# Queries and keys of an attention layer transposed on VectorE, ahead of time, instead of on TensorE when they are used

## The chip, the cores and the metric

The kernel runs on one core of a Trainium2 chip. The metric is the device time of one execution in microseconds; the time of a kernel is the median of its runs. Five engines work side by side, each through its own instructions in order: TensorE (PE in the profile, PEld its weight loads), VectorE (DVE), ScalarE (ACT), GpSimd (POOL) and SyncE (SP), which here issues nearly all DMA transfers. Semaphores make an engine wait for another or for a transfer.

## The reference

One layer of a hybrid model, 16 meta tokens ahead of 1024 tokens of width 1024. One input projection feeds three mixers: a short convolution, a latent attention with 8 heads (MLA), and a retention with 4 heads. An output projection and a residual end the layer. Only the attention's queries and keys are touched by the change:

```python
def mla_mixer(c_q, c_kv, k_rope, z, q_a_norm, w_uq, kv_a_norm, w_ukv, q_norm, k_norm, cos, sin):
    q = (rms_norm(c_q, q_a_norm) @ w_uq).reshape(B, L, MLA_HEADS, QK_HEAD)          # QK_HEAD = 96
    ...
    k = jnp.concatenate([k_nope, k_r], axis=-1)
    q = rms_norm(q, q_norm)
    k = rms_norm(k, k_norm)
    q = jnp.concatenate([q[..., :QK_NOPE], apply_rope(q[..., QK_NOPE:], cos, sin)], axis=-1)
    k = jnp.concatenate([k[..., :QK_NOPE], apply_rope(k[..., QK_NOPE:], cos, sin)], axis=-1)
    ...
        s = jnp.einsum('bqhd,bkhd->bhqk', qb, k).astype(jnp.float32) * scale
        mask = cid[None, :] <= qc[:, None]
        s = jnp.where(mask[None, None], s, neg)
        p = jax.nn.softmax(s, axis=-1).astype(v.dtype)
        return jnp.einsum('bhqk,bkhd->bqhd', p, v)
    ...
    return o * jax.nn.silu(z)

u = rms_norm(h, ln_w[l])
(cx, cb, cc, cz, cq, ckv, krope, mz, rq, rk, rv, rz) = jnp.split(u @ w_in[l], IN_OFFSETS, axis=-1)
y = jnp.concatenate([y_conv, y_mla, y_ret], axis=-1)
h = h + y @ w_out[l]
```

## The kernel before, in words

Precision: every large product is made of three fp32r matmuls (`mm3`, L112) of high and low halves. `split` (L103 to L107) makes the halves: ScalarE writes the high one, VectorE (for some weights GpSimd) the low one by subtraction.

The program goes through units, each a block of columns of the input projection with eight weight chunks (`load_w`, L118: a DMA of 256 KB into one of three staging buffers, then a split):
- `mz`, the gate of the attention, in the opening (0 to 55 us), while the input arrives in pieces (`xs`) and is split. The row norms of the tokens come from ScalarE's sums of squares; `rps` (L243) spreads them over the partitions by a matmul with `dg`, once for each half of the tokens. The gated blocks `mzz` are stored to `mz_s` (L260).
- `A`, the latents of the attention (58 to 123 us): for each of nine tiles of tokens it makes q, k (`kqo`) and v, norms and rotates them, and stores them to HBM, token by token, in `q_s`, `k_s` (L388, L368) and `v_s`.
- `r0` and `r1`, the retention (120 to 246 us): nine tiles of tokens each. `r_proj` makes the projection, `r_rope` rotates on VectorE (`qk`), `r_score` makes the scores `rsp` on TensorE, which VectorE decays into `qs` (L478), and updates the running `state`; `r_out` (L494) multiplies `qs` on TensorE into `rop`. `later` and `step` put each part one tile behind the one before it, so that tile t's projection stands between the parts of tiles t-1, t-2 and t-3.
- `c0` and `c1`, the convolution (246 to 343 us).
- the attention (from 325 us, mixed with the end of c1): 8 heads of 8 query tiles. `score` makes S and its row maxima, `p_t` transposes the probabilities, `attend` multiplies them by v; `partial` does the first quarter of the output projection between them.
- the output projection's end (531 us on).

Queries and keys return in pairs of heads: `load_pair` (L546, L547) gathers 768 KB each of q and k, still one token to a partition. S needs them with the 96 features of a head on the partitions, so `qk_t` transposes them on TensorE, four transposes of 128 tokens (L668) into a PSUM tile, and splits that tile into `qT` or `kT`; the scale `wqk` (the product of the two norms' weights) is applied to q there. `qk_t` is called two heads ahead, four times a head: two halves of the tokens, q and k.

A scheduler sets the order of each engine's instructions from the order of the code and its own estimates of time; once built the order is fixed. Buffers come from pools: the pool of q, k and `kqo` tiles has two buffers for each tag, and a tile waits until the one two before it under its tag has been used.

## Time and profile before

| | us |
|---|---|
| median of 3 runs | 580.92 |
| lowest and highest | 580.18, 584.61 |
| profiled execution, its own time | 581.55 |
| its span | 579.8 |
| TensorE busy | 569.8 (98%) |
| VectorE busy | 330.9 (57%) |
| ScalarE busy | 255.0 (44%) |
| GpSimd busy | 224.1 (39%) |

The profile is of one execution; its span leaves out what lies before the first and behind the last instruction. The granted TensorE clock is at full speed in all 40 slices of the page. A row of the timeline gives start, length, engine, line, operation, the tile written and the tiles read, how many instructions were joined in the row, and in brackets how long the engine had been idle before and what ended that.

### The profile page before, as it was taken

What the parts mean: (1) busy time and instruction counts of PE and PEld (TensorE: products, weight loads), DVE (VectorE), ACT (ScalarE), POOL (GpSimd) and SP (SyncE); (2) the same over time, 40 slices, a digit from 0 to 9 for tenths busy, and PEclk for the clock granted to TensorE, in tenths of its full rate; (3) what the DMA queues carried; (4) which work ended last, traced back from release to release, by engine and by line L of the source; (5) the groups of instructions that cost most, each with busy time, mean ns of one, the idle gap of its engine ahead of it and who ended that gap; (6) DMA issues with size and microseconds to landing.
All of it is one profiled execution on the core that took longest, in us unless ns stands there. A gap on an engine that the chain in (4) does not pass through costs nothing.

```text
span 579.8 us, 9595 instructions
## 1 busy us (share of the span) xinstructions
PE 569.8 (98%) x3401; PEld 481.7 (83%) x3401; DVE 330.9 (57%) x761; ACT 255.0 (44%) x616; POOL 224.1 (39%) x330
## 2 busy tenths in 40 slices
PE   8999999999999999999999999999999999999997
PEld 5877899988888888898898888898888888876886
DVE  5547768888536432553332667675757857664132
ACT  6765535665234332532010438475655646543000
POOL 2023258677103220151242968443524334624000
PEclk9999999999999999999999999999999999999999
DMA  8887513274703200130030648235112223113096
GB/s 326 289 265 241 182 67 120 108 224 158 234 1 92 74 0 19 54 110 18 20 97 1 199 145 273 73 103 171 56 38 73 77 71 128 37 68 116 1 301 224
DMA packets 46657, 70.39 MB, mean 121 GB/s; under 512 B 3792, under 2 KB 21840, under 8 KB 46480
## 3 DMA queue, kind: packets, MB, share of 16 engines
q1 hardware_dynamic: 43008, 63.47, 33.8%
q10 hardware_dynamic: 3600, 6.29, 2.9%
q8 instruction: 27, 0.44, 0.3%
q14 instruction: 22, 0.18, 0.1%
HBM read 48.75 MB, written 21.00 MB: 120 GB/s over the span
## 4 chain that ended last, share of the span: by engine, by line
PE 83%; DMA 9%; DVE 3%; ACT 2%; issue 2%; POOL 0%; SPq 0%; DVEq 0%; ACTq 0%; POOLq 0%
PE r L112 16%; PE S L112 9%; PE cv L112 8%; PE part L112 7%; PE A L112 6%; PE o L765 6%; PE pTp L724 5%; PE cz L112 4%; PE cb L112 4%; DMA out<-ot 4%; PE out L112 3%; PE qps L112 3%; DMA xs<-in_xT 2%; DMA xt<-in_x 2%; PE rsp L477 1%
## 5 line engine op out<-in xcount | busy, mean ns | idle before, releaser
L702 ACT ACTIVATE pr<-S,smx 128x144 f32<-128x144 f32 (+8 forms) x72 | 50.4, 701 | 27.3 <-DVE smx L693 13.4
L693 DVE TENSOR_REDUCE smx<-S 128x1 f32<-128x144 f32 (+8 forms) x72 | 49.8, 701 | 15.7 <-PE S L112 6.3
L710 POOL TENSOR_SCALAR pm<-pr,smx 128x16 f32<-128x16 f32 x64 | 18.4, 288 | 85.2 <-DVE smx L708 61.3
L711 POOL TENSOR_SCALAR pr<-pr,smx 128x128 f32<-128x128 f32 (+3 forms) x64 | 48.1, 752 | 0.6 <-DVE smx L708 0.6
L724 PE MATMUL pTp<-ident,pr 128*128 128x128 f32 x288 | 45.4, 274 | 1.5 <-ACT pt L730 1.4
L730 ACT COPY pt<-pTp 128x512 f32<-128x512 f32 (+2 forms) x64 | 31.8, 505 | 26.3 <-PE pTp L724 24.9
L451 POOL TENSOR_SCALAR kw<-qk,con 128x64 f32<-128x64 f32 (+1 forms) x36 | 13.8, 397 | 71.7 <-DVE qk L447 58.4
L724 PEld LDWEIGHTS pTp<-ident,pr 128*128 128x128 f32 x288 | 35.0, 140 | 7.0 <-POOL wol L104 1.8
L765 PEld LDWEIGHTS o<-pt,v 128*64 128x64 f32 x448 | 26.5, 137 | 12.1 <-issue 4.7
L765 PE MATMUL o<-pt,v 128*64 128x256 f32 (+2 forms) x448 | 36.2, 309 | 0.0
L112 PE MATMUL r<-wh_r,xal 128*128 128x512 f32 (+1 forms) x80 | 30.5, 381 | 0.0
L112 PE MATMUL r<-wh_r,xah 128*128 128x512 f32 (+1 forms) x80 | 30.4, 380 | 0.0
L112 PE MATMUL part<-woh,yh 128*128 128x512 f32 x64 | 30.1, 470 | 0.0
L112 PE MATMUL r<-wl_r,xah 128*128 128x512 f32 (+1 forms) x80 | 30.0, 375 | 0.0
L882 DVE SCALAR_TENSOR_TENSOR ot<-out,xr 128x512 f32<-128x512 f32 (+1 forms) x17 | 11.2, 660 | 31.1 <-DMA out<-ot 16.8
L112 PE MATMUL r<-wl_r,xbh 128*128 128x512 f32 x64 | 26.1, 409 | 0.0
L112 PE MATMUL r<-wh_r,xbh 128*128 128x512 f32 x64 | 25.7, 401 | 0.0
L112 PE MATMUL part<-wol,yh 128*128 128x512 f32 x64 | 25.5, 399 | 0.0
L112 PE MATMUL r<-wh_r,xbl 128*128 128x512 f32 x64 | 25.5, 398 | 0.0
L112 PE MATMUL part<-woh,yl 128*128 128x512 f32 x64 | 25.2, 394 | 0.0
L773 DVE TENSOR_TENSOR ym<-o,ym 64x256 f32<-64x256 f32 x32 | 13.5, 421 | 16.7 <-PE o L767 16.2
L104 POOL TENSOR_TENSOR wol<-wos,woh 128x512 fp32r<-128x512 f32 x16 | 20.4, 1291 | 2.6 <-ACT woh L103 2.6
(295 smaller groups left out, 1716.1 us busy)
## 6 DMA issues: line engine op xcount, KB each, us to landing
xt<-in_x SPq DMA_DIRECT2D x16, 256.0 KB, 4.5
ws_r<-in_win SPq DMA_DIRECT2D x16, 256.0 KB, 3.3
ws_c<-in_win SPq DMA_DIRECT2D x16, 256.0 KB, 2.9
wos<-in_wout SPq DMA_DIRECT2D x16, 256.0 KB, 3.8
xp<-in_x SPq DMA_DIRECT2D x16, 256.0 KB, 2.7
p_s<-xp SPq DMA_DIRECT2D x16, 256.0 KB, 2.0
xr<-p_s SPq DMA_DIRECT2D x15, 256.0 KB, 4.5
out<-ot ACTq DMA_DIRECT2D x15, 256.0 KB, 4.5
```

The costliest lines, as they stand in the source:

```text
L104: (lo_eng or nc.vector).tensor_tensor(lo, src, hi.bitcast(F32), op=ALU.subtract)
L112: nc.tensor.matmul(out, lhsT=x_, rhs=y_, start=first and i == 0, stop=last and i == 2)
L451: nc.gpsimd.tensor_scalar(kw[R, j], qk[R, 2 + j], con[R, kd0 + j:kd0 + j + 1], 1.0, op0=ALU.mult, op1=ALU.mult)
L693: nc.vector.tensor_reduce(sm[:, i // 2:i // 2 + 1], sp[:, :n, :w], axis=AX.XY, op=ALU.max, negate=True)
L702: e = nc.scalar.activation(pr[:, c0:c1].rearrange("p (b c) -> p b c", b=n), sp, AF.Exp, bias=mx, accum_out=sm[:, 5 + i:6 + i])
L710: nc.gpsimd.tensor_scalar(pm[(2 * h + t // 4) % 2][:, t % 4, :NM], pr[:, nk - NM:nk], sm[:, 9:10], 1.0, op0=ALU.mult, op1=ALU.mult)
L711: nc.gpsimd.tensor_scalar(pr[:, :nk - NM], pr[:, :nk - NM], sm[:, 9:10], 1.0, op0=ALU.mult, op1=ALU.mult)
L724: tr_ = nc.tensor.transpose(out=tp[:, b * P:b * P + P], in_=pr[:, c0:c0 + P], identity=ident)
L730: nc.scalar.copy(pt[:, b0:b0 + nb, tt], src)
L765: nc.tensor.matmul(op[64 * cg:64 * cg + 64, c0:c1], lhsT=lv, rhs=src[:, i_, c_], start=b == 0, stop=False)
L773: nc.vector.tensor_tensor(ys, op[64 * cg:64 * cg + 64, :256].rearrange("p (a c q) -> p a c q", a=2, q=64), ys, op=ALU.mult)
L882: nc.vector.scalar_tensor_tensor(ot, acc[:, c0:c1], 0.5, xt, op0=ALU.mult, op1=ALU.add)
```

## The change

Queries and keys are turned in HBM, between the A unit and the attention. `turn(i, part)` handles pair i // 2, keys for even i and queries for odd. It has three parts, and the loop over the retention's 18 tiles calls one part after each tile but the meta tiles: part 0 loads 768 KB token by token from `k_s` or `q_s` (`ts`); part 1 is one VectorE instruction that transposes the tile's 32x32 blocks (`td`, 128 x 1536 elements); part 2 scales it, for q alone, with two ScalarE activations, and stores it as one contiguous piece of 768 KB in `T_s`. Part 2 of a turn is called with part 0 of the next. Before the attention and then a head ahead, `load_head` reads one head's q and k, three DMAs of 128 KB each, with the features on the partitions; `qk_t` is then only a split from SBUF. `load_pair` loads v alone.

The opening: the rows `rps` are made for both halves after both groups' norms (`r_row`); the matmuls of `rest(2, 1)` are cut into chunks 0 to 5 ahead of them and 6, 7 behind; the last four A weight loads are called inside the loop over the gated blocks; there are 11 warm-up matmuls instead of 8 (`NW`). `wqk` has a second column, since a partition now holds 32 features of each of three blocks.

```diff
-    NA, NW, GA = 4, 8, 0
+    NA, NW, GA = 4, 11, 0
...
+            if g == GA:
+                rest(2, 1, accs[2, 1], range(6))
             if g == 2:
                 break
+
+        def r_row(g):
...
-        rest(2, 1, accs[2, 1])
+        for g in range(2):
+            r_row(g)
+        rest(2, 1, accs[2, 1], range(6, KT))
         for g in range(2):
             accs[3, g] = ps0.tile([P, 512], F32, tag="rps", name=f"mz3{g}", bufs=2)
-            rest(3, g, accs[3, g])
+        for k in range(KT):
+            for g in range(2):
+                rest(3, g, accs[3, g], (k,))
         for b in range(4):
+
+            with tc.issue_after(last_t.ins):
+                wA.append(load_w("A", len(wA)))
...
-        wA += [load_w("A", k) for k in range(len(wA), KT)]
...
+    def turn(i, part):
+
+        hp, which = i // 2, 1 - i % 2
+        if part == 0:
+            src = hp_pool.tile([P, NT, 192], F32, tag="q", name=f"ts{i}")
+            nc.sync.dma_start(src, (q_s, k_s)[which].rearrange("t p c -> p t c")[:, :, hp * 192:hp * 192 + 192])
+            turned.append(src)
+        elif part == 1:
+            dst = hp_pool.tile([P, 6, NT * 32], F32, tag="q", name=f"td{i}")
+            nc.vector.transpose(dst.rearrange("p c (t k) -> p t c k", k=32),
+                                turned.pop().rearrange("p t (c k) -> p t c k", k=32))
+            turned.append(dst)
+        else:
+            dst = turned.pop()
+            if which == 0:
+
+                for c in range(2):
+                    nc.scalar.activation(dst[:, c::3], dst[:, c::3], AF.Copy, scale=wqk[:, c:c + 1])
+            nc.sync.dma_start(T_s[which][hp], dst.rearrange("p c r -> p (c r)"))
+
     for u in range(2):
         for t in [8] + list(range(NT)):
             r_proj(u, t)
             step()
+            if t != 8:
+                i, part = divmod(u * NT + t, 2)
+                if part == 0 and i:
+                    turn(i - 1, 2)
+                turn(i, part)
...
+    def load_head(h):
+        for which in (1, 0):
+            x = hp_pool.tile([P, 1536], F32, tag="qk"[which], name=f"{'qk'[which]}{h}")[:96, :SEQ]
+            src = T_s[which][h // 2].rearrange("(i f) (c r) -> c f i r", i=4, c=6)
+            for c in range(3):
+                nc.sync.dma_start(x[32 * c:32 * c + 32].rearrange("p (i r) -> p i r", i=4), src[3 * (h % 2) + c])
+            raw[h, which] = x.rearrange("p (i t k) -> p t i k", i=4, k=32)
+
     def load_pair(hp):
-        qt = hp_pool.tile([P, NT, 192], F32, tag="q", name=f"q{hp}")
-        kt = hp_pool.tile([P, NT, 192], F32, tag="k", name=f"k{hp}")
         vt = hp_pool.tile([P, NT, 128], F32, tag="v", name=f"v{hp}")
-        nc.sync.dma_start(kt, k_s.rearrange("t p c -> p t c")[:, :, hp * 192:hp * 192 + 192])
-        nc.sync.dma_start(qt, q_s.rearrange("t p c -> p t c")[:, :, hp * 192:hp * 192 + 192])
...
+    turn(NT - 1, 2)
+    for h in range(2):
+        load_head(h)
     pairs = [load_pair(0)]
...
         def qk_t(h, g, which):
-            qt, kt, _ = pairs[h // 2]
-            cs = slice(96 * (h % 2), 96 * (h % 2) + 96)
-            tp = pst("tq", f"{'qk'[which]}Tp{h}_{g}")
-            src = (qt, kt)[which]
-            for j in range(4):
-                nc.tensor.transpose(out=tp[:96, j * P:j * P + P], in_=src[:, 4 * g + j, cs], identity=ident)
...
+            src = raw[h, which][:, 4 * g:4 * g + 4]
+            o = g * 512 + NM * which
+            dst = [x[:96, o:o + 512].rearrange("p (t i k) -> p t i k", i=4, k=32) for x in (qT, kT)[which][h % 2]]
...
+            split(*dst, src)
...
+    load_head(2)
     cuts = [load_wo(k, 1) for k in (0, 1, 6, 7)]
...
+            if t == 5 and h + 3 < H:
+                load_head(h + 3)
```

Three places of the order, as the two programs are built. SyncE at the change from the A unit to the retention, before (`ws_r` is the last chunk of r1's weights, `ws_c` are chunks of c0's):

```order
L388 DMA q_s<-kqo_1642 128x768
L548 DMA v_3652<-v_s 128x8x128
L368 DMA k_s<-kqo_1642 128x768
L547 DMA q_3277<-q_s 128x8x192
L547 DMA q_3650<-q_s 128x8x192
L118 DMA ws_r_1931<-in_win 128x512
L118 DMA ws_c_2456<-in_win 128x512
```

and in the changed program, the same place:

```order
L400 DMA q_s<-kqo_1647 128x768
L380 DMA k_s<-kqo_1647 128x768
L543 DMA ts_1729<-k_s 128x8x192
L556 DMA kT_s<-td_1784 128x1536
L543 DMA ts_1843<-q_s 128x8x192
L543 DMA ts_2012<-k_s 128x8x192
L556 DMA qT_s<-td_1901 128x1536
L556 DMA kT_s<-td_2079 128x1536
L543 DMA ts_2145<-q_s 128x8x192
L543 DMA ts_2313<-k_s 128x8x192
L556 DMA qT_s<-td_2203 128x1536
L120 DMA ws_r_1945<-in_win 128x512
L120 DMA ws_c_2494<-in_win 128x512
```

Between the last store of keys and r1's last weight chunk nine transfers of the turns now stand; the loads of q and k by pairs are gone.

VectorE in r0, before (the numbers in `rup_1`, `rsp_1` are the tiles of the retention):

```order
L447 TENSOR_TENSOR qk_2_1816<-qk_2_1816 128x256
L489 SCALAR_TENSOR_TENSOR state_1574<-state_1574,con,rup_1_1810 64x64 x2
L478 TENSOR_TENSOR qs_1_1771<-rsp_1_1805,con 128x256
L444 TENSOR_TENSOR qk_3_1872<-rt_3_1870,con 128x256
L445 TENSOR_TENSOR qk_3_1872<-rt_3_1870,con 128x4x32
L446 TENSOR_TENSOR qk_3_1872<-rt_3_1870,con 128x4x32
L468 SCALAR_TENSOR_TENSOR zsb_0_1721<-zsb_0_1721,rt_3_1870 128x128
L447 TENSOR_TENSOR qk_3_1872<-qk_3_1872 128x256
L478 TENSOR_TENSOR qs_2_1827<-rsp_2_1861,con 128x256
L489 SCALAR_TENSOR_TENSOR state_1574<-state_1574,con,rup_2_1866 64x64 x2
```

and in the changed program:

```order
L459 TENSOR_TENSOR qk_3_1884<-qk_3_1884 128x256
L547 STREAM_TRANSPOSE td_1901<-ts_1843 128x8x6x32
L501 SCALAR_TENSOR_TENSOR state_1579<-state_1579,con,rup_2_1878 64x64 x2
L490 TENSOR_TENSOR qs_2_1836<-rsp_2_1873,con 128x256
```

The second transpose stands ahead of the state update of tile 2 and of its qs.

VectorE at the end of r1's weights, before:

```order
L104 TENSOR_TENSOR wl_r_1928<-ws_r_1925,wh_r_1927 128x512
L478 TENSOR_TENSOR qs_5_2054<-rsp_5_2095,con 128x256
L104 TENSOR_TENSOR wl_r_1934<-ws_r_1931,wh_r_1933 128x512
L489 SCALAR_TENSOR_TENSOR state_1574<-state_1574,con,rup_5_2100 64x64 x2
L104 TENSOR_TENSOR wl_c_2459<-ws_c_2456,wh_c_2458 128x512
```

and in the changed program:

```order
L106 TENSOR_TENSOR wl_r_1942<-ws_r_1939,wh_r_1941 128x512
L490 TENSOR_TENSOR qs_5_2073<-rsp_5_2116,con 128x256
L547 STREAM_TRANSPOSE td_2375<-ts_2313 128x8x6x32
L106 TENSOR_TENSOR wl_r_1948<-ws_r_1945,wh_r_1947 128x512
L456 TENSOR_TENSOR qk_7_2186<-rt_7_2184,con 128x256
```

The fifth transpose stands right ahead of the low half of r1's last weight chunk.

## Rows read from the trace of the kernel before

**Rows 1.** The page, part 1 (busy time, share, instructions) and part 4 (the chain)
```profile
PE 569.8 (98%) x3401; PEld 481.7 (83%) x3401; DVE 330.9 (57%) x761; ACT 255.0 (44%) x616; POOL 224.1 (39%) x330
...
PE 83%; DMA 9%; DVE 3%; ACT 2%; issue 2%; POOL 0%; SPq 0%; DVEq 0%; ACTq 0%; POOLq 0%
```

**Rows 2.** The table of windows: stretch, its length, then each engine's busy time
```profile
core 0: us, PE busy (x) PEld busy (x) DVE busy (x) ACT busy (x) POOL busy (x), PEclk, DMA share, GB/s
6.00:58.70 52.70, 50.50 (x218) 39.88 (x218) 34.41 (x58) 35.45 (x76) 12.02 (x11) 1.00 0.84 282
148.00:181.00 33.00, 33.00 (x168) 27.50 (x167) 12.85 (x42) 11.12 (x32) 5.37 (x10) 1.00 0.24 77
398.50:422.00 23.50, 23.50 (x186) 19.94 (x188) 15.68 (x39) 13.24 (x34) 9.57 (x19) 1.00 0.25 79
510.00:531.50 21.50, 20.05 (x166) 15.63 (x165) 10.54 (x25) 10.65 (x23) 8.81 (x10) 1.00 0.26 88
```

**Rows 3.** The table of lines, forms apart: L668, the transposes of the queries
```profile
L668 PE MATMUL qTp<-ident,q 128*96 128x128 f32 x64 | 9.6, 273 | 0.0
```

**Rows 4.** The timeline of TensorE, one group of transposes and what follows
```profile
413.05 0.60 PE L668 MATMUL qTp<-ident,q 128*96 128x128 f32 x4
413.43 0.47 PE L112 MATMUL S<-kt1h,qt1h 104*128 104x456 f32 x1
```

**Rows 5.** The chain of work that ended last: start, length, what
```profile
14.10 6.00 DMA xs<-in_xT
...
346.20 0.88 PE kTp L668 x8
```

**Rows 6.** The timeline of VectorE, start of the attention
```profile
332.45 3.08 DVE L579 SCALAR_TENSOR_TENSOR yv<-ccs,vec,yv 128x512 f32<-128x512 f32 x1
```

**Rows 7.** The table of lines, forms apart: two reductions on VectorE
```profile
L381 DVE TENSOR_REDUCE sqq<-qsq 128x8 f32<-128x768 f32 x8 | 7.5, 940 | 0.2 <-ACT qsq L375 0.2
...
L352 DVE TENSOR_REDUCE sk<-ksq 128x8 f32<-128x512 f32 x8 | 5.4, 677 | 2.9 <-ACT ksq L349 2.9
```

**Rows 8.** DMA issues: count, KB each, median us from issue to landing
```profile
k_s<-kqo SPq DMA_DIRECT2D x8, 384.0 KB, 2.3
...
q<-q_s SPq DMA_DIRECT2D x4, 768.0 KB, 6.9
...
k<-k_s SPq DMA_DIRECT2D x4, 768.0 KB, 5.5
...
xr<-p_s SPq DMA_DIRECT2D x2, 128.0 KB, 3.7
```

**Rows 9.** The timeline of SyncE's queue, 148 to 182 us
```profile
148.00 0.32 SPq L368 DMA_DIRECT2D k_s<-kqo  x1
...
181.59 0.35 SPq L118 DMA_DIRECT2D ws_r<-in_win  x1
```

**Rows 10.** The timeline of TensorE in the retention unit
```profile
165.99 0.33 PE L494 MATMUL rop<-rt,qs 128*128 128x64 f32 x2
...
172.63 0.45 PE L494 MATMUL rop<-rt,qs 128*128 128x64 f32 x3
...
180.71 0.44 PE L494 MATMUL rop<-rt,qs 128*128 128x64 f32 x3
...
189.44 0.28 PE L112 MATMUL r<-wl_r,xah 128*16 128x256 f32 x1
```

**Rows 11.** The timeline of VectorE in the retention unit
```profile
161.32 0.43 DVE L478 TENSOR_TENSOR qs<-rsp,con 128x256 f32<-128x256 f32 x1 [1.74 <-PE rsp L477]
```

**Rows 12.** The timeline of TensorE and, second row, VectorE in the opening
```profile
5.96 0.80 PE L112 MATMUL mz<-xah,wh_mz 128*128 128x512 f32 x1 [1.18 <-ACT wh_mz L103]
...
44.00 0.69 DVE L244 COPY rb<-rps 128x512 f32<-128x512 f32 x1 [1.20 <-PE rps L243]
...
58.12 0.24 PE L112 MATMUL A<-wh_A,xah 128*16 128x160 f32 x1 [1.51 <-ACT wh_A L103]
...
58.74 0.25 PE L112 MATMUL A<-wl_A,xah 128*16 128x160 f32 x1 [0.38 <-DVE wl_A L104]
```

More of the change, by code (lines that the diff above doesn't have):

```diff
@@ L77, in trunk @@
     v_s = dp.tile([L, 512], F32, name="v_s")
+    T_s = [dp.tile([4, P, 1536], F32, name=f"{c}T_s") for c in "qk"]
     mz_s = dp.tile([4, P, SEQ], F32, name="mz_s")
@@ L177, in trunk, with rest @@
         nc.scalar.activation(acts, half_neg[:, :1], AF.Tanh)
[L179 to L180 removed]
+        def rest(b, g, a, ks=range(KT)):
+            for k in ks:
                 mm3(a, [w[:, b * P:b * P + P] for w in wmz[k]], X(k, NM + g * 512, 512), k == 0, k == KT - 1)
```

32 lines of the change are left out of this document (13 added, 19 removed).

## The prediction

> **What bounds the kernel now.** I read the page first. TensorE is busy for 98% of the span, and the chain of work that ended last runs through it for 83%, with DMA 9% and VectorE 3% behind [rows 1]. A share of busy time is a mean over stages, so the table of windows came next. From 148 to 181 us, in the retention unit, TensorE is busy for all 33.00 us while VectorE has 12.85; in one head's period of the attention, 23.5 us, TensorE has all 23.5 and VectorE 15.68. It is short of work in the opening (50.50 of 52.70 us) and at the last heads (20.05 of 21.50) [rows 2]. So between these two ends a microsecond taken from TensorE is a microsecond of the total, and whatever the change hands to VectorE is free until TensorE waits for it.
>
> **The transposes that go (-13.1).** There are 128, 64 of queries and 64 of keys; the row of the queries stands in [rows 3], that of the keys differs by 1 ns. The table of lines gives each 273 ns, which would make 128 x 0.273 = 34.9 us. These durations overlap, though: a matmul's record runs until its result has drained, and the next starts before that. What one costs is the distance of starts. In the timeline four transposes start at 413.05 and the S matmul behind them at 413.43: 0.38 / 4 = 0.095 us each [rows 4]. The chain gives a group of eight 0.88 us, 0.11 each [rows 5]. So 128 x 0.095 = 12.2 us at the low end and 128 x 0.11 = 14.1 at the high one. I take the middle, 13.1. All of it lies in windows in which TensorE has no gap, so all of it counts.
>
> The row's 273 ns agrees with what the Trainium skill, page "TensorE: Matmul & The Clock Gate", section "Part 4: PE-mode transpose", gives for a transpose in a kernel's context, about 275 ns; taken as a cost, that would make the gain 128 x 0.275 = 35 us. The starts in this trace speak against using it so.
>
> With the transposes go the reads of PSUM by the two halves of the split, and the scale moves to ScalarE, 8 activations in the retention unit, where it is busy for 11.12 of 33 us [rows 2]. Both engines have spare time in every window named, so I cost this at nothing. What that rests on is VectorE's 7.8 spare microseconds a head. SBUF-only operations can be held: one 128x512 operation took 3.08 us at 332.45 [rows 6], against 0.68 for a reduction of that shape [rows 7]. Two such a head would still fit.
>
> **The VectorE transposes that come.** Eight, 128 x 1536 elements each. No row shows the operation. The nearest are reductions over elements that go by once: 677 ns for 512 a partition, 940 ns for 768 [rows 7]. The slope is 263 / 256 = 1.03 ns an element, so 1536 elements make 940 + 768 x 1.03 = 1.73 us. For the low end I take half of that, 0.9; for the high end twice, 3.5, about what the held operation of [rows 6] shows can happen to a VectorE operation. I take 1.75, as the same engine reading the same type of data in one pass is the nearest.
>
> Eight times 1.75 is 14 us of VectorE in a stretch where it has 20 of 33 idle. What matters is what waits for them. Each turn is a chain: load 768 KB, transpose, store 768 KB, and since the pool has two buffers for it, the next load starts only when the transpose before it has read its source. A load of this size landed in 5.5 us for k and 6.9 for q [rows 8]. I price a load alone at 5.5, and one with the store of the turn before beside it at 7.4. The last k rows are stored at 148.00 [rows 9]; the first load can start about 150.5 (2.3 us for a store of this size [rows 8]). With T = 1.75 the transposes end at 150.5 + 5.5 + 1.75 = 157.8, then 166.9 (7.4 + 1.75 on), 174.2, 183.3, 190.6, 199.7.
>
> VectorE takes its instructions in order, and the order puts the second transpose ahead of the decayed queries qs of step 2 and the fifth right ahead of the low half of r1's last weight chunk. SyncE does the same: that chunk's load stands behind nine of the new transfers. Who needs them: TensorE multiplies qs of step 2 at 165.99, of step 3 at 172.63, of step 4 at 180.71 (so a step is 7.36 us), and the last weight chunk's low half at 189.44 [rows 10]. VectorE had qs of step 2 done at 161.75 [rows 11], 4.2 us early.
> - Step 2: the transpose ends at 166.9, the state update and qs behind it add about 1.0, so 167.9 against 165.99: 1.9 us of stall.
> - Step 3: 174.2 + 0.4 against 172.63 + 1.9 = 174.5: 0.1.
> - The last chunk: 190.6 + 0.7 for the low half = 191.3 against 189.44 + 2.0 = 191.4: none.
> - Step 6 behind the sixth transpose: about 0.5, of the same kind.
>
> That is 2.5; a chain of eight whose loads differ as those of k and q do will lose a little more, and I take **+3.0**. At T = 0.9 the same working gives about 0.5. At T = 3.5 the ends are 159.5, 170.4, 179.4, 190.3, 199.3, 210.2: 5.4 at step 2, 1.8 at step 3, 3.4 at the chunk, 2.2 at step 6, together **13**.
>
> **The opening (-1.0).** TensorE waits 1.51 us for the last A chunk and 0.38 for its low half [rows 12]. That load stands on SyncE behind five stores of the gated mz blocks, and by the order it still does. What can move is the fifth store: VectorE lost 1.20 us on the way to it, waiting for the second row of rps [rows 12], and with both rows made together this wait goes; TensorE's order now has matmuls of the second tile ahead of the low half, which hides the 0.38. Against that, the first row now waits for the second group's sums too, so the first blocks start later. The most is 1.9, and 2.2 is all of TensorE's idle time from 6 us on, 52.70 - 50.50 [rows 2]; the least is a loss of about 1, if the later start is passed on. I take 1.0 of gain, a little over half. Three more warm-ups cover the 1.18 us ahead of the first mz matmul [rows 12] and I give them nothing: TensorE is caught again behind an xs load that takes from 14.10 to 20.10 [rows 5].
>
> **Entry of the attention (+0.6).** Each head's q and k are now six loads of 128 KB a head ahead, 48 instead of the eight loads of pairs; each takes SyncE some 0.4 us to issue, as the issue at 148.00 does (0.32) [rows 9]. In a head's period that is 2.4 us of a queue that has 23.5 us. At the entry they stand ahead of other loads, and VectorE's splits of the second head come before TensorE's first out-projection fills. The bounds are nothing and one landing of 128 KB in full, 3.7 us [rows 8]; nearer to nothing, as the data was stored some 100 us before: 0.6.
>
> **The sum.** -13.1 - 1.0 + 3.0 + 0.6 = -10.5. The profiled execution took 581.55, so 571.05; the median of the three runs is 0.63 lower, at 580.92: **570.4**.
>
> **The rivals.**
> 1. *The chain hides altogether.* T near 0.9, or loads at their quickest, and the A waits gone: -13.1 - 1.9 + 0.5 = 566. For it: VectorE idles 20 us of 33 and the DMA engines are nearly idle there. Against: the stall at step 2 comes out at 1.9 even with the middle price.
> 2. *The gain is eaten in the retention unit.* T = 3.5, or turns of 10 us instead of 8.4: -13.1 - 1.0 + 13 + 0.6, about 580. For it: no row prices this operation, and by my own prices two turns take 7.25 + 9.15 = 16.4 us against 14.7 for two steps. The Trainium skill speaks for it, page "VectorE: DVE Perf Modes": its section "The three transpose paths" has 311 ns for a 128x128 bf16 on VectorE, of which twelve are one of these, an estimate of 3.7 us; and its "Rules for kernel authors" send a 128x128 transpose to TensorE. Against: the reductions run at one element in 1.03 ns.
> 3. *Slower.* If VectorE needs 5 us for one transpose, each turn is 11.5 us or more against a step of 7.36, and the ends are 161.0, 173.4, 183.9, 196.3, 206.8: TensorE idles for 8.4 us at step 2, 3.3 at step 3, 6.4 at the chunk and some 4 behind it, as the conv unit's weights stand in the same SyncE queue: -13.1 - 1.0 + 22 + 0.6 = +8.5, 589. It decides from T = 3.6 on, where the stalls pass 13.5. Against: nearly three times the reductions' price.
> 4. *The transposes weren't on the path.* Then VectorE or ScalarE must end the heads, with 15.7 and about 13 us of 23.5. It would be about 582. The windows speak against it.
> 5. *The record is the price.* If a transpose cost TensorE its record's 273 ns, the gain would be 34.9 and the time 548. Against: the starts [rows 4], where four take 0.38 us and not 1.09.
>
> **How the numbers follow.** The forecast, 567 to 575, has 0.51; the first rival 0.2 (562 to 567); the second 0.18 (575 to 584); the third 0.07; the fourth 0.03; the last 0.01. The measurement tells about 1% from no change, 5.8 us here. Faster than 575.1: 0.51 + 0.2 + 0.01 and a hair of the second's, 0.73. Within 1%: the rest of the second and the fourth, 0.2. Slower than 586.7: 0.07. The range leaves out the third rival and the ends of the first and second: 562.5 to 581.
>
> **What would show it.** In the changed profile: no L668-like transposes, and heads about 1.6 us shorter than 23.5, the sixteen transposes' 16 x 0.1025. STREAM_TRANSPOSE of 1.7 to 1.8 us, eight times, 7 to 9.5 us apart. TensorE waits of about 2 us released by VectorE's qs between 160 and 175, and small ones at r1's last chunk. No wait for wh_A at 58. It is wrong if one transpose takes over 3 us, if a head's period doesn't shrink, or if TensorE waits for a weight chunk queued behind the turns for more than 3 us.

## The result and the profile after

The changed kernel takes 583.62 us (median; lowest 581.22) against 579.7 for the kernel before in the same comparison: a ratio of 1.0058, 95% interval 1.0039 to 1.0077. Each was run twenty times; two runs of the changed kernel, of 619 and 1409 us, are left out of the ratio. It is 0.6% slower, where 1.8% faster was forecast. The profiled execution took 585.29 us with a span of 583.5 (before: 581.55 and 579.8).

The page of the changed kernel, busy time and the chain; it answers to [rows 1]:

```profile
PE 568.4 (97%) x3276; PEld 472.7 (81%) x3276; DVE 353.4 (61%) x769; ACT 261.4 (45%) x624; POOL 229.0 (39%) x330
...
PE 72%; DVE 11%; DMA 8%; ACT 4%; issue 3%; POOL 2%; SPq 0%; DVEq 0%; ACTq 0%; POOLq 0%
```

TensorE is busy for 1.4 us less, not 13, and the chain now runs through VectorE for 11% instead of 3%. Busy time isn't work here: the mean granted clock of this execution is 0.991 (before: 1.000), and the three stretches at a lower clock shown below cost TensorE some 5 us.

The places where the time went are found with five marks on TensorE: the first matmul of the retention (`r`), of the convolution (`cv`), and the first S of heads 0, 2 and 7 (the form 104x144 is a head's first query tile). The kernel before, timeline of TensorE:

```profile
121.36 0.28 PE L112 MATMUL r<-wh_r,xah 128*16 128x256 f32 x1
...
245.62 0.28 PE L112 MATMUL cv<-xah,wh_c 128*128 128x258 f32 x1
...
331.17 0.31 PE L112 MATMUL S<-kt0h,qt0h 104*128 104x144 f32 x1
...
379.41 0.31 PE L112 MATMUL S<-kt0h,qt0h 104*128 104x144 f32 x1
...
496.75 0.23 PE L112 MATMUL S<-kt1h,qt1h 104*128 104x144 f32 x1
```

and the changed kernel, the same five:

```profile
121.68 0.28 PE L114 MATMUL r<-wh_r,xah 128*16 128x256 f32 x1
...
251.21 0.28 PE L114 MATMUL cv<-xah,wh_c 128*128 128x258 f32 x1
...
335.09 0.23 PE L114 MATMUL S<-kt0h,qt0h 104*128 104x144 f32 x1
...
389.24 0.23 PE L114 MATMUL S<-kt0h,qt0h 104*128 104x144 f32 x1
...
504.50 0.31 PE L114 MATMUL S<-kt1h,qt1h 104*128 104x144 f32 x1
```

The last matmul stage, `out`, starts at 531.4 before and 535.4 after. The distances between marks, with the forecast's terms put to the same stretches (of the 128 transposes the trace of before has 16 ahead of the S mark of head 0, 36 between those of heads 0 and 2, and 76 between those of heads 2 and 7, at 0.1025 each):

| stretch | before | after | difference | forecast |
|---|---|---|---|---|
| start to `r` | 121.4 | 121.7 | +0.3 | -1.0 |
| `r` to `cv` (retention) | 124.3 | 129.5 | +5.3 | +3.0 |
| `cv` to S of head 0 | 85.6 | 83.9 | -1.7 | -1.6 |
| S of head 0 to head 2, and S of head 7 to `out` | 82.9 | 85.0 | +2.1 | -3.1 |
| S of head 2 to S of head 7 | 117.3 | 115.3 | -2.1 | -7.8 |
| sum | | | +4.0 | -10.5 |

The first two and the last head stand in one row, because the order shifts work between them: the first stretch has 64 attend matmuls before and 88 after, the last one 128 and 104. Two stretches hold 11 of the 14.5 us that the forecast missed: the entry of the attention, and the steady heads, which kept 2 of 8 us.

**What came as forecast.** The table of lines has the new operation, and the timeline of VectorE five of the eight:

```profile
L547 DVE STREAM_TRANSPOSE td<-ts 128x1536 f32<-128x1536 f32 x8 | 14.2, 1776 | 19.2 <-DMA ts<-q_s 12.7 <-DMA qT_s<-td 3.7 <-DMA ts<-k_s 2.8
```

```profile
155.55 1.78 DVE L547 STREAM_TRANSPOSE td<-ts 128x1536 f32<-128x1536 f32 x1 [2.76 <-DMA ts<-k_s]
...
164.03 1.78 DVE L547 STREAM_TRANSPOSE td<-ts 128x1536 f32<-128x1536 f32 x1 [3.98 <-DMA ts<-q_s]
...
172.48 1.78 DVE L547 STREAM_TRANSPOSE td<-ts 128x1536 f32<-128x1536 f32 x1 [1.89 <-DMA qT_s<-td]
...
181.09 1.78 DVE L547 STREAM_TRANSPOSE td<-ts 128x1536 f32<-128x1536 f32 x1 [3.50 <-DMA ts<-q_s]
...
190.04 1.76 DVE L547 STREAM_TRANSPOSE td<-ts 128x1536 f32<-128x1536 f32 x1
```

One takes 1.776 us (1.75 was taken from [rows 7]), and they end at 157.3, 165.8, 174.3, 182.9 and 191.8 where the working had 157.8, 166.9, 174.2, 183.3 and 190.6. Three of the five brackets say that VectorE waits for a load, the third names the store of the turn before, and the fifth has no wait, because VectorE itself was late; so the first four ends are set by the transfers.

The page "VectorE: DVE Perf Modes" of the Trainium skill, section "The three transpose paths", gives 311 ns for a 128x128 bf16 on VectorE, which was the estimate of 3.7 us in the second rival. The trace has 1.776 for the twelve, so an estimate of twelve times the page's figure is too high for one large fp32 instruction, and the slowdown needs no dear transpose.

**The retention.** The wait came at step 5, not at step 2. The timeline of the changed kernel, all engines, 182 to 191 us:

```profile
182.90 0.72 ACT L555 ACTIVATE td<-td,wqk 128x512 f32<-128x512 f32 x1 [3.63 <-DVE so L520]
...
183.65 0.69 ACT L450 ACTIVATE rt<-r,r 128x512 f32<-128x512 f32 x1
...
184.44 0.42 DVE L456 TENSOR_TENSOR qk<-rt,con 128x256 f32<-128x256 f32 x1 [1.52 <-ACT rt L450]
...
185.95 1.41 POOL L525 TENSOR_TENSOR rwk<-rwk,zsb 128x512 f32<-128x512 f32 x1 [1.30 <-DVE rwk L524]
...
186.12 1.79 DVE L106 TENSOR_TENSOR wl_r<-ws_r,wh_r 128x512 fp32r<-128x512 f32 x1
...
187.83 1.35 DVE L480 SCALAR_TENSOR_TENSOR zsb<-zsb,rt 128x128 f32<-128x128 f32 x1
...
189.70 0.41 DVE L490 TENSOR_TENSOR qs<-rsp,con 128x256 f32<-128x256 f32 x1
...
190.17 0.66 PE L506 MATMUL rop<-rt,qs 128*128 128x64 f32 x4 [1.88 <-DVE qs L490]
```

Read it from the last row back. TensorE waits 1.88 us for `qs` of VectorE. `qs` comes at 189.70, since the instructions ahead of it on VectorE are late and long: a low half of r1's weights takes 1.79 us while GpSimd works beside it (185.95), where the next one, at 189.10, takes 0.68, and `zsb` takes 1.35. They are late because VectorE's `qk` waited 1.52 us for ScalarE's copy `rt` of the projection, and that copy stood behind the scale of the second query turn (182.90), whose transpose (181.09 to 182.87, above) had waited for its load. (The bracket of the scale names `so`, VectorE's instruction behind that transpose.) The windows of the same stretch:

```profile
core 0: us, PE busy (x) PEld busy (x) DVE busy (x) ACT busy (x) POOL busy (x), PEclk, DMA share, GB/s
188.00:190.00 2.00, 0.29 (x3) 0.10 (x1) 2.00 (x3) 0.00 (x0) 2.00 (x3) 1.00 0.80 265
190.00:192.00 2.00, 1.83 (x14) 1.54 (x15) 2.00 (x3) 1.21 (x2) 0.17 (x1) 0.87 0.56 173
192.00:194.00 2.00, 2.00 (x8) 1.36 (x7) 1.96 (x7) 1.53 (x4) 0.00 (x0) 0.50 0.99 339
194.00:196.00 2.00, 2.00 (x9) 1.62 (x8) 1.46 (x4) 0.92 (x3) 0.88 (x2) 0.77 0.93 208
```

In the first TensorE is busy for 0.29 of 2 us; in the three after it the granted clock is 0.87, 0.50 (the 1.2 GHz level) and 0.77, while TensorE has all the work it can do. In this execution the wait is paid a second time. That isn't so each time: eight of the kernels below have the same retention code (e2, e4, e6, e7, e9, e11, e13, e16), and in their traces it takes 127.6 to 128.7 us, with a lower clock in e7 alone. Of the +5.3 at most 1.9 us are therefore the clock's, and +3.4 to +4.4 is there without it.

**The entry of the attention.** Timeline of VectorE, GpSimd and TensorE:

```profile
325.57 0.68 DVE L106 TENSOR_TENSOR qt0l<-q,qt0h 96x512 fp32r<-96x512 f32 x1
...
330.23 3.60 DVE L106 TENSOR_TENSOR kt0l<-k,kt0h 96x512 fp32r<-96x512 f32 x1
...
330.62 2.55 POOL L106 TENSOR_TENSOR wol<-wos,woh 128x512 fp32r<-128x512 f32 x2
...
337.80 0.68 DVE L607 TENSOR_TENSOR ccs<-cv,rb 128x512 f32<-128x512 f32 x1
...
338.54 0.79 PE L114 MATMUL cz<-xbh,wh_c 128*128 128x512 f32 x1 [2.57 <-DVE ccs L607]
```

```profile
336.00:340.00 4.00, 1.47 (x4) 1.18 (x5) 4.00 (x5) 1.28 (x3) 2.17 (x3) 0.78 0.94 262
340.00:344.00 4.00, 4.00 (x16) 3.20 (x15) 3.31 (x8) 1.76 (x5) 4.00 (x4) 0.79 1.11 236
```

VectorE's splits of q and k no longer follow TensorE's transposes, so they run as soon as their loads land, ahead of `ccs` (they fill VectorE from 330.23 to 337.88), and one takes 3.60 us beside GpSimd's subtractions. TensorE waits 2.57 us for `ccs`, and the granted clock is 0.78 and 0.79 in the two windows around and behind the wait. The page "GPSIMD Engine Reference" of the Trainium skill, section "Specifications", says that GpSimd's access to this memory (SBUF) is shared with VectorE and that VectorE's instructions with two inputs there contend; the 3.60 against the 0.68 of the same operation at 325.57, where GpSimd only cleared tiles, agrees.

**The opening.** The wait that should have gone is there (table of waits; us, times, longest), with a slow window behind it:

```profile
PE A L114 <- ACT wh_A L105: 2.2, 1, 2.2
```

```profile
58.00:62.00 4.00, 4.00 (x16) 3.75 (x15) 2.53 (x5) 2.39 (x4) 0.00 (x0) 0.57 0.90 318
```

### The profile page after: what moved, and what is told of

The parts are those of the page before. It is cut to its first block, busy times and chain, and to the rows that moved or that the text cites. A ratio compares the mean times of both kernels' runs of the same rounds, so it can differ in the third digit from the quotient of the medians.

```text
span 583.5 us, 9444 instructions
## 1 busy us (share of the span) xinstructions
PE 568.4 (97%) x3276; PEld 472.7 (81%) x3276; DVE 353.4 (61%) x769; ACT 261.4 (45%) x624; POOL 229.0 (39%) x330
## 4 chain that ended last, share of the span: by engine, by line
PE 72%; DVE 11%; DMA 8%; ACT 4%; issue 3%; POOL 2%; SPq 0%; DVEq 0%; ACTq 0%; POOLq 0%
PE S L114 9%; PE r L114 8%; PE out L114 8%; PE part L114 7%; PE A L114 6%; PE cv L114 6%; PE o L805 6%; PE pTp L764 5%; PE cz L114 4%; PE cb L114 4%; PE qps L114 2%; DMA ts<-q_s 2%; DMA xs<-in_xT 2%; DMA xt<-in_x 2%; PE mz L114 1%
## 5 line engine op out<-in xcount | busy, mean ns | idle before, releaser
L750 POOL TENSOR_SCALAR pm<-pr,smx 128x16 f32<-128x16 f32 x64 | 20.3, 317 | 82.9 <-DVE smx L748 71.1
L805 PE MATMUL o<-pt,v 128*64 128x256 f32 (+2 forms) x448 | 38.4, 311 | 0.0
L547 DVE STREAM_TRANSPOSE td<-ts 128x1536 f32<-128x1536 f32 x8 | 14.2, 1776 | 19.2 <-DMA ts<-q_s 12.7
```

The lines of the kernel that those rows point to most:

```text
L547: nc.vector.transpose(dst.rearrange("p c (t k) -> p t c k", k=32), turned.pop().rearrange("p t (c k) -> p t c k", k=32))
L750: nc.gpsimd.tensor_scalar(pm[(2 * h + t // 4) % 2][:, t % 4, :NM], pr[:, nk - NM:nk], sm[:, 9:10], 1.0, op0=ALU.mult, op1=ALU.mult)
L805: nc.tensor.matmul(op[64 * cg:64 * cg + 64, c0:c1], lhsT=lv, rhs=src[:, i_, c_], start=b == 0, stop=False)
```

## The experiments

The theory: TensorE still sets the pace, and the gain is lost where work that used to follow TensorE's transposes now runs earlier in the in-order engines and stands ahead of something that TensorE needs (in the retention, at the entry, in the heads), each wait being made longer by the lower clock behind it. The first rival, W: the transposes were never on the path, so that taking them away gives nothing anywhere. The second: the new transfers and VectorE's transposes cost what is missing. "Ratio" is to the kernel before of the same comparison, with its 95% interval; stretches are those of the table above.

**e1, the kernel before with one of four transposes** (each result is used for all four 128-token blocks, so the attention of the other tokens is not computed).

```diff
-            for j in range(4):
-                nc.tensor.transpose(out=tp[:96, j * P:j * P + P], in_=src[:, 4 * g + j, cs], identity=ident)
+            nc.tensor.transpose(out=tp[:96, :P], in_=src[:, 4 * g, cs], identity=ident)
+            tp = tp[:96, None, :P].to_broadcast([96, 4, P])
...
```

> The kernel before, with one of every four transposes of q and k left: the first 128 tokens of each half stand for all four (so the attention of the other tokens is not computed). 96 transposes go, the splits still read PSUM, nothing is added. Theory P (TensorE sets the pace of the heads and each transpose costs its distance of starts): 96 x 0.1025 = 9.8 us less, about 570. Rival W (a head's pace is set by the loop score, softmax on ScalarE, GpSimd's scaling, transposes of the probabilities; with less work TensorE waits for it): 0 to 5 us less, 575 to 580, with waits of TensorE at pTp and S that the kernel before doesn't have.

Ratio 1.0011 (0.9994 to 1.0028): 96 transposes fewer, and no gain, which looks like W. The stretches say more: the steady heads take 115.0 us, as in the changed kernel, and the first and last heads 86.6, 3.7 more than before. The table of waits has the wait behind that, and the timeline of GpSimd where it starts:

```profile
PE qTp L667 <- DVE qt1l L107: 5.8, 1, 5.8
```

```profile
343.10 0.70 POOL L614 TENSOR_SCALAR wos<-wos,vec 128x512 f32<-128x512 f32 x1 [5.47 <-DMA wos<-in_wout]
```

GpSimd waits 5.47 us for out-projection weights, VectorE's `yv` waits for GpSimd's, and `qt1l` stands behind `yv` in VectorE's order. SyncE issues that load at 336.67, behind a load of keys of 768 KB at 336.25; in the kernel before the weights go first (333.76, the keys at 336.99) and GpSimd has no such wait.

Neither VectorE's transposes nor new transfers are in this kernel, so they aren't needed for the loss in the heads. But its splits still follow TensorE's transposes, so the theory as stated doesn't cover it: TensorE waits 1.7 us for ScalarE in its five heads, and why the rest of the saving is missing there stays open.

**e7, the changed kernel with 128 transposes put back on TensorE**, of data that nobody reads.

```diff
+            tp = pst("tq", f"{'qk'[which]}Tp{h}_{g}")
+            for j in range(4):
+                nc.tensor.transpose(out=tp[:96, j * P:j * P + P], in_=ident[:, :96], identity=ident)
             split(*dst, src)
```

> The changed kernel with TensorE's 128 transposes put back as work without use: four transposes of a constant ahead of each split, whose result nobody reads. Theory W (in the heads TensorE waits anyway, the transposes fill waits): within 3 us of the changed kernel. Rival P (TensorE sets the pace): 128 x 0.1025 = 13 us slower, about 597.

Ratio 1.0264 (1.0244 to 1.0285), 12 us over the changed kernel: the heads 121.2 (+5.9), the first and last 88.6 (+3.6), `cv` to S +1.6. Put in, 128 transposes cost 12 us, 0.094 each, near what the forecast said, so W falls as a general explanation. Taking them out and putting them in aren't opposite, then; the runs below ask whether it is the order that comes with it.

**e2, the kernel before's opening in the changed kernel.**

```diff
-    NA, NW, GA = 4, 11, 0
+    NA, NW, GA = 4, 8, 0
...
-                rest(2, 1, accs[2, 1], range(6))
...
+        wA += [load_w("A", k) for k in range(len(wA), KT)]
```

> The changed kernel with the opening of the kernel before (8 warm-ups, rows made one by one, A loads behind). Theory: the new opening gives nothing, since the earlier start of the A unit (53.6 against 54.9) is lost again to a wait of 2.2 us for the last A chunk and to the halved clock from 58 to 62 us behind it; so the same time within 1 us. Rival, the forecast's term: 1 us slower without it. Rival on the other side: 1 us or more faster, if the halved clock costs more than the reordering gives.

Ratio 1.0048 (1.0015 to 1.0080), not told apart from the changed kernel's 1.0058. The opening brings nothing that these intervals can show, either way.

**e3, the scale of q left out of the turns** (so q's norm weights are not applied).

```diff
-                for c in range(2):
-                    nc.scalar.activation(dst[:, c::3], dst[:, c::3], AF.Copy, scale=wqk[:, c:c + 1])
```

> The changed kernel without the two ScalarE activations that scale a turned q (the scale of q is left out). Theory S (ScalarE's in-order wait is the cause of the stall at step 5 of r0: the scaling of the fourth turn waits for its transpose to end at 182.9 and holds the copy rt of tile 6, behind which VectorE then makes qs of step 5 late): the wait of 1.9 us for qs and the halved clock behind it go, 3 to 5 us faster. Rival T (the transpose itself, late on VectorE behind its load, is enough): qs of step 5 comes less than 1 us earlier, TensorE still waits and its clock still falls, less than 1.5 us faster.

Ratio 1.0035 (1.0016 to 1.0055). The retention takes 127.2, against 127.6 to 129.5 in the changed kernel and the eight with the same retention code. The wait for `qs` at step 5, 0.9 to 1.9 us in those nine, isn't there. So ScalarE's scale was a link of that chain, as its row at 182.90 says, but without it smaller waits of TensorE, 1.6 us in all, remain.

**e5, turns with buffers of their own, and each transpose called three tiles behind its load instead of one.**

```diff
-            dst = hp_pool.tile([P, 6, NT * 32], F32, tag="q", name=f"td{i}")
+            dst = hp_pool.tile([P, 6, NT * 32], F32, tag="k", name=f"td{i}")
...
-                turn(i, part)
+                turns(u * NT + t)
```

> The changed kernel with the turns pipelined: the loads ts take their buffers from another tag than the transposed pieces td, and a turn's transpose is called two steps behind its load and not one. Theory (the retention unit loses 5.3 us because VectorE's and ScalarE's in-order queues wait for a turn whose load is late): the waits of VectorE for ts go from 12 to 19 us to under 3, TensorE doesn't wait at step 5, the first cv comes at 246 and not at 251; 4 to 6 us faster than the changed kernel, about 578. Rival (the 64 transfers themselves, or VectorE's 14 us, hold the unit up, through r1's and c0's weight loads): less than 1.5 us faster.

Ratio 1.0117 (1.0075 to 1.0159). The retention is back at 124.3, but `cv` to S takes 87.9, 4.0 more, with a wait of 1.5 us for GpSimd's `rwk` at 252.75; by the edit the last turns are now called among c0's matmuls. Here the delay moved the loss and didn't remove it.

**e10, VectorE's transposes, the scales and the stores kept behind the last `qs` in the order.**

```diff
+            pin[0] = nc.vector.tensor_tensor(qs[:, 2:], sp, DT[:, 2 * u:2 * u + 2], op=ALU.mult).ins
...
+                    with tc.issue_after(pin[0]):
+                        turn(i - 1, 2)
```

> The changed kernel with each turn's transpose, scaling and store held behind VectorE's qs of the step in which they are called, so that a turn takes two steps (14.7 us) and its load has landed when VectorE comes to it. Theory (VectorE's and ScalarE's in-order waits for late loads cost the retention unit 5.3 us): r to cv takes 124 to 126 us and not 129.5, no transposes wait for ts more than 1 us, 3 to 5 us faster than the changed kernel. Rival (the later turns then stand among c0's weight halves and the loss comes back at cv, as it did when the turns were pipelined): within 1.5 us of it.

Ratio 0.9996 (0.9969 to 1.0022), retention 124.3. The windows of 188 to 192 us, where the changed kernel lost most:

```profile
188.00:190.00 2.00, 2.00 (x20) 1.82 (x18) 1.66 (x6) 1.31 (x4) 0.83 (x2) 1.00 0.88 325
190.00:192.00 2.00, 2.00 (x11) 1.56 (x10) 1.25 (x3) 1.40 (x3) 0.21 (x1) 1.00 0.41 109
```

TensorE is busy for all of it at a granted clock of 1.00. The eight transposes and all their transfers are still there, so the whole loss of the retention was place in the order, and the second rival falls for this stretch. The trace also holds a test of the clock at the entry: `cz` waits 2.6 us for `ccs` as in the changed kernel, and the clock stays at 1.00.

```profile
334.00:338.00 4.00, 4.00 (x19) 3.29 (x18) 3.34 (x8) 1.75 (x5) 4.00 (x4) 1.00 1.05 273
```

Yet S of head 0 to S of head 2 takes 54.2 us, as in the changed kernel (54.1), and TensorE waits 1.3 us more, for VectorE's `yv`. So the clock doesn't set the length of the entry.

**e4 and e6, the splits moved later.** e4 calls those of head 0's second half and of head 1 behind the exponentials; e6 spreads them over the query tiles, one each. **e8** is e5 and e6 together.

```diff
-    qk_t(0, 1, 1)
-    qk_t(0, 1, 0)
     score(0, 0)
...
+    with tc.issue_after(late["act"]):
+        qk_t(0, 1, 1)
+        qk_t(0, 1, 0)
```

```diff
-    QK = (3, 3, 4, 4)
+    QK = (3, 4, 5, 6)
...
```

> The changed kernel with six of the splits of the first two heads (the second half of head 0, all of head 1) called behind the first scores, so that on VectorE they stand behind the convolution's ccs. Theory: the wait of 2.6 us of cz for ccs and the halved clock from 338 to 342 go, 3 to 5 us faster. Rival: the splits then stand ahead of the first row maxima of S and TensorE waits there for as long, within 1 us of the changed kernel.

> The changed kernel with the splits of the heads spread: those of head 1 one by one in the first four steps of the attention, behind that step's softmax, and those of later heads in steps 3, 4, 5, 6 of a head and not two each in 3 and 4. Theory (splits that stand in VectorE's and ScalarE's queues ahead of ccs and of row maxima make TensorE wait): the wait of cz for ccs goes, 3 to 4 us, and a head's period falls from 23.6 to 23.0 or less; 4 to 8 us faster than the changed kernel. Rival (the loop over scores, softmax, scaling on GpSimd and transposes of the probabilities sets the heads' pace however the splits stand): 3 to 4 us faster, from the entry alone, and the heads' period stays.

> Both edits together, turns pipelined and splits spread. If the two losses are separate, the gains add: 8 to 14 us faster than the changed kernel, 570 to 576, the first version below the kernel before. Rival: they don't add, since a wait that goes in one place comes back at the next; 576 to 582.

Ratios 1.0131 (1.0097 to 1.0165), 1.0119 (1.0092 to 1.0146) and 1.0105 (1.0042 to 1.0168): misses. In e4 the wait for `ccs` is gone, but TensorE then waits 3.2 us for GpSimd's probability row, and the first and last heads take 88.6; in e6 88.3. The timeline of GpSimd in e4 has what that row stood behind:

```profile
345.53 1.61 POOL L662 TENSOR_SCALAR wos<-wos,vec 128x512 f32<-128x512 f32 x1 [4.19 <-DMA wos<-in_wout]
```

It is the wait of e1 again, for out-projection weights that SyncE issues (341.53) behind three loads of keys (340.14); e6 has it with 2.15 us, the changed kernel with 0.99. With the splits out of the way, the next wait is the transfers' place in SyncE's order. e8 shows no sum of gains; it too is slower than the kernel before.

**e9, each attend in one run on TensorE**, not mixed with transposes of probabilities.

```diff
+                    with tc.issue_after(late.get("o", late["act0"])):
                         tr_ = nc.tensor.transpose(out=tp[:, b * P:b * P + P], in_=pr[:, c0:c0 + P], identity=ident)
...
+                      with tc.issue_after(late["pe"]):
                         nc.tensor.matmul(op[64 * cg:64 * cg + 64, c0:c1], lhsT=lv, rhs=src[:, i_, c_], start=b == 0, stop=False)
```

> The changed kernel with the matmuls of each attend kept in one run on TensorE: held behind the last transpose of the probabilities called before them, and the next transposes held behind them. In the order of the changed kernel o and pTp change places 41 times, in that of the kernel before 9 times, here 23. Theory (in the heads the changed kernel loses again what the transposes gave, about 0.8 us a head, because such a change costs TensorE about 0.13 us more than staying, besides waits of pTp): 3 to 6 us faster than the changed kernel, heads of 22.8 or less. Rival (the changes of place are harmless, the waits of pTp alone cost): within 1.5 us of it.

Ratio 1.0014 (0.9989 to 1.0040), heads 113.3 against 115.3. By the starts in the changed kernel's five heads, waits left out, from one transpose of probabilities to the next takes 0.12 us and from one attend matmul to the next 0.07, but from a transpose to an attend 0.23 and back 0.21. The kernel before has none of these switches in the five heads, the changed one 28, e9 15: thirteen fewer at some 0.13 each are 1.6 of the 2.0 us that the heads gain here.

**e11, copies of the mask moved from VectorE to ScalarE at the entry; e12, the edits of e9, e10 and e11 together.**

```diff
-        nc.vector.tensor_copy(qT[i][0][96:104], msk[96:104, :SEQ])
+        nc.scalar.copy(qT[i][0][96:104], msk[96:104, :SEQ])
...
```

> The changed kernel with the four copies of the masks into qT and kT (4 us of VectorE at 326 to 330, while GpSimd clears the same tiles) on ScalarE. Theory (cz waits 2.6 us because VectorE's queue ahead of ccs is too long by that much): the wait and the halved clock behind it go, 3 to 4 us faster than the changed kernel. Rival (VectorE is held by GpSimd's work however the copies stand): the wait stays over 1.5 us, less than 1.5 us faster.

> The three edits together (attends in one run, turns held, copies on ScalarE). If each loss is a place of its own, 9 to 14 us faster than the changed kernel: 570 to 575, 1 to 1.6% below the kernel before. Rival: the losses trade places, 577 to 582.

Ratios 1.0100 (1.0062 to 1.0139) and 0.9991 (0.9955 to 1.0027). The wait for `ccs` goes, but the first and last heads take 87.5 and 89.2: TensorE waits for GpSimd's probabilities (0.9 and 2.0 us) and VectorE's `yv` (2.3) instead, and behind both stands GpSimd's wait for out-projection weights (2.23 and 2.78), whose loads stand among the heads' loads on SyncE.

**e13, loads of heads 1 and 2 and the splits of head 1 kept behind the load of `vr`; e14, e12 and e13 together; e15, e14 with the last A chunk loaded through ScalarE's queue.**

```diff
-    for h in range(2):
-        load_head(h)
+    load_head(0)
...
+    with tc.issue_after(vrl.ins):
+        load_head(1)
```

> The changed kernel with the loads of heads 1 and later held on SyncE behind the last load of vr, so that the out-projection's chunks wos go first, and head 1's splits behind them. Theory (at the entry the head loads wait on SyncE for VectorE's splits, since they need their buffers, and hold wos behind them; GpSimd then waits for wos ahead of the scaling of the first probabilities): from the end of the convolution to the first o falls from 10.7 us or stays while the convolution ends 4 us earlier, 4 to 8 us faster than the changed kernel. Rival (the start of the attention is set by the splits on VectorE, wherever the loads stand): the first o doesn't come earlier than at 361, within 2 us of the changed kernel.

> Attends in one run, turns held, mask copies on ScalarE, and head loads behind vr. Theory (retention, entry and heads each lose at a place of their own, and the entry's place was SyncE's queue): 570 to 575, 1 to 2% below the kernel before. Rival (the entry is bounded by something that none of the edits moves): 578 to 583.

> The same, and the last A chunk loaded through ScalarE's queue, past the stores of the gated mz blocks. Theory: the wait of 1.9 to 2.7 us at 56 us and the halved clock behind it go, 2 to 4 us less than with the four edits. Rival: ScalarE comes to the load as late, as it waits for the staging buffer; no difference over 1 us.

Alone it is the worst of the new orders, 1.0171 (1.0142 to 1.0201): head 1's data come late, ScalarE's splits of it stand ahead of a probability copy, and TensorE's timeline and windows show what follows:

```profile
364.05 0.98 PE L763 MATMUL pTp<-ident,pr 128*128 128x128 f32 x7 [3.36 <-ACT pt L769]
```

```profile
364.00:368.00 4.00, 3.39 (x16) 2.37 (x16) 2.96 (x8) 4.00 (x10) 2.06 (x2) 0.73 0.78 196
368.00:372.00 4.00, 2.48 (x11) 2.00 (x10) 2.62 (x6) 2.36 (x7) 3.30 (x7) 0.50 0.86 244
```

A wait of 3.36 us, and granted clocks of 0.73 and 0.50 behind it. With e12's edits it is a gain, the first and last heads taking 85.5 us instead of e12's 89.2: e14 0.9964 (0.9942 to 0.9986), e15 0.9970 (0.9942 to 0.9997), the same. e14's heads still take 113.2 us, and once a head the timeline of ScalarE (`kt0h`, `qt0h` are splits of a later head) and TensorE reads like this:

```profile
400.87 0.62 ACT L105 CAST kt0h<-k 96x512 fp32r<-96x512 f32 x1 [0.27 <-PE S L114]
...
401.50 0.61 ACT L105 CAST qt0h<-q 96x512 fp32r<-96x512 f32 x1
...
402.02 0.61 ACT L105 CAST kt0h<-k 96x512 fp32r<-96x512 f32 x1
...
402.66 0.58 ACT L778 COPY pt<-pTp 128x512 f32<-128x512 f32 x1
...
403.30 0.33 PE L772 MATMUL pTp<-ident,pr 128*128 128x128 f32 x1 [0.73 <-ACT pt L778]
```

Three casts, free to run since their data lie in SBUF, stand ahead of the copy `pt` that frees the buffer TensorE waits for. Before, each could only follow its own transposes on TensorE.

**e16, each split kept behind a tile's copy `pt` on ScalarE, alone; e17, the same with e14's edits.**

```diff
-    QK = (3, 3, 4, 4)
+    QK = (4, 5, 6, 7)
...
+                    late["ptc"] = nc.scalar.copy(pt[:, b0:b0 + nb, tt], src).ins
...
+                    with tc.issue_after(late["ptc"]):
+                        qk_t(h + 2, *((0, 1), (0, 0), (1, 1), (1, 0))[i])
```

> The changed kernel with one edit: in the heads, the four splits of a later head's q and k are called one each at query tiles 4 to 7, and each is kept behind ScalarE's copy of that tile's transposed probabilities. Theory (the splits no longer depend on TensorE, so ScalarE's order has up to three of them ahead of a copy that TensorE waits for): four heads take about 92 us instead of the changed kernel's 94.1, and the time comes to about 578 to 580 in a call where the kernel before has 581. Rival (the alternation of attends and probability transposes alone makes the heads long): the heads stay at 94 and the time at 583 to 585.

> The four edits of e14 together with the held splits of e16. Theory: the one wait of 0.7 to 1.0 us a head that e14 still shows, of TensorE for ScalarE's probability copy behind three casts, goes, and four heads take 88 to 89 us instead of e14's 91.3, which is the kernel before's 94.25 less its 64 transposes at 0.1 to 0.11; the time comes to 572 to 574, a ratio near 0.987. Rival (the casts take ScalarE's time in any place, so the wait moves on to another copy): 91 us and 578, a ratio of 0.996.

e16: 1.0076 (1.0044 to 1.0107), no gain alone: its five heads take 117.4 us, in turn some 21 and 25 each, with 30 of the switches between attends and transposes. e17: 575.53 us, **0.9897 (0.9870 to 0.9924)**, faster than both kernels. Its marks on TensorE:

```profile
243.09 0.28 PE L114 MATMUL cv<-xah,wh_c 128*128 128x258 f32 x1
...
326.92 0.23 PE L114 MATMUL S<-kt0h,qt0h 104*128 104x144 f32 x1
...
383.08 0.23 PE L114 MATMUL S<-kt0h,qt0h 104*128 104x144 f32 x1
...
493.13 0.23 PE L114 MATMUL S<-kt1h,qt1h 104*128 104x144 f32 x1
```

The five heads take 110.0 us, 7.3 less than before, against the forecast's 7.8, and TensorE's table of waits has no row between 380 and 500 us. e14, without the held splits, has 113.2, 2.9 of it waits for `pt`, so the held splits are what removes them. Retention: 124.2. `cv` to S: 83.8. No run has e17's order with the transposes put back, so how much of the 7.3 us is the transposes and how much a better order isn't separated.

## Why the prediction was wrong

**The step that failed** is the sentence on the transposes, "All of it lies in windows in which TensorE has no gap, so all of it counts". The price was near right and the conclusion wasn't. With the order mended (e17) the kernel takes 1.7 us less from `cv` to S of head 0 and 7.3 less in the five steady ones, 9.0 of the 9.4 forecast there; in the changed kernel as built the same stretches give 3.8. Put back (e7), the 80 transposes of these stretches cost 7.6. A TensorE without a gap shows that work on it can't be hidden; it doesn't show that the gap left by removed work closes. The other engines' instructions were in step because they waited for those transposes. Without them, ScalarE and VectorE took up the splits early, in front of copies that TensorE waits for (shown by e14's row and by e17), and the attends were cut up among other matmuls (e9). The five heads take 117.3 us before, 115.3 after, 113.3 in e9 and 110.0 in e17. In the changed kernel itself TensorE's waits in them are only 1.4 us; the 28 switches, at some 0.13 each, are the greater part. That the freed splits are what made the scheduler cut up the attends is argued, not shown: e1, with fewer transposes but the splits tied to them, has one switch.

**"Both engines have spare time in every window named, so I cost this at nothing"** failed for the same reason. The time was spare, but an in-order engine's spare time isn't a place in its order. The 3.08 us operation of [rows 6] was noted, and 3.60 came ahead of `ccs`, which TensorE waited for.

**The entry (+0.6)** was mis-sized most: with the 36 transposes that were to go, the first and last heads were to give -3.1 and gave +2.1. Set against the -3.7 of these transposes the entry lost 5.8 us, and its upper bound was 3.7. The changed kernel's trace shows a wait of 2.57 us and a lower clock behind it (0.22 and 0.21 of 4 us each, 1.7 us). But e10 is as long there at a clock of 1.00, and without that wait (e4, e6, e11, e12) TensorE waits for GpSimd and VectorE instead, which stand behind loads of out-projection weights. The prediction said that the heads' loads stand ahead of other loads, and priced that near nothing. e17 doesn't mend the entry: its first and last heads take 86.6, with waits of 1.5 us for a split of head 1 and several under 1. What an order would have to be in which the entry gives its 3.7 us stays open.

**The retention (+3.0)** was the right kind of stall with the wrong place and size: +5.3 in the profiled execution, +3.4 to +4.4 in the kernels with the same code, at step 5. The prediction followed VectorE and SyncE and left out ScalarE, whose scale stood ahead of the projection's copy (e3), and had no term for the clock: 0.13, 0.50 and 0.23 of 2 us each between 190 and 196, 1.7 us. e10 shows that the place in the order is all of it. The named stall of 1.9 us at step 2 didn't come: the second transpose ended 1.1 us earlier than worked out, `qs` was there at 166.7, and TensorE came to `rop` at 167.04 and not at 165.99. The 7.4 us for a load with a store beside it stood on no row; loads of the turns landed in 4.8 (k) and 6.3 (q), by the median.

**The opening (-1.0)** gave +0.3. The wait for the last A chunk, 1.5 us before, is 2.2; in e2 it is 2.6 and in e15 2.1, and neither gains. The stretch from the first A to the first `r` takes from 65.8 us (e17) to 69.8 (e6) with the same code of the opening, so a term of 1 us was below what it varies by.

**Right** were the price of a transpose on TensorE by the distance of starts, T, the chain's ends, and the naming of the second rival, "The gain is eaten in the retention unit". That rival's range, 575 to 584, holds the measured time by luck: its mechanism (T of 3.5 us) wasn't the one, and the retention, 2.3 us over the forecast, was a sixth of the miss.

## What to carry to other kernels

When work is taken off the bound engine, ask what its results were holding back: every instruction that depended on it becomes free, and in a fixed order it may now stand ahead of something that the bound engine needs. Count a saving in full only when the neighbours' places are kept, with an explicit order if need be, and judge such a change by the time between marks in a steady stretch, not by the engine's busy share. An edit that is right alone can measure as nothing or a loss (e16, e13) until the next wait behind it is also removed.

## What the runs showed of the hardware that was not expected

- A TensorE wait of 2 to 3 us is often followed by a stretch at a lower granted clock while TensorE is fully busy: 0.57 at 58 to 62 us after 2.2 us, 0.50 at 192 to 194 after 1.88, 0.78 and 0.79 after 2.57. It isn't certain: 3.2 us in the opening of e13 and 2.6 us at the entry of e10 left the clock at 1.00. At step 5 of the retention it fell behind 1.88 us (changed kernel) and 1.78 (e7), and stayed at 1.00 behind 1.41 to 1.75 us in six kernels (e4, e6, e9, e11, e13, e16).
- A VectorE subtraction of 96x512 with both inputs in SBUF took 0.68 us while GpSimd cleared tiles and 3.60 beside GpSimd's subtractions.
- A switch on TensorE between a transpose and an attend matmul takes 0.21 to 0.23 us from start to start (mean over the changed kernel's five heads), against 0.07 to 0.12 within a run of one kind.
